# Differential attention on one core: the combination of the two exponentials of a unit made wholly by VectorE, none of it by GpSimd

## The chip, the cores and the metric

One Trainium2 chip, one of its cores. The time is that of one execution on the device, in microseconds (us); of several runs the median is given. The engines of the core are named TensorE (PE in the profile), VectorE (DVE), ScalarE (ACT), GpSimd (POOL) and SyncE (SP, which here only issues DMAs).

## The reference

Two layers; each mixes 512 latent tokens (and 256 context tokens) by three groups side by side: a recurrent one, a short convolution, and differential attention of four heads, whose part alone matters here. One input projection feeds all groups, one output projection takes their gated outputs. The attention has two score maps per head (j), of 64 channels each, and a number `lam` for each layer; behind it come a norm over the 128 channels of v and the gate:

```python
def diff_attend(q, k, v, lam, scale):
    s = jnp.einsum('bqhjd,bkhjd->bhjqk', q, k).astype(jnp.float32) * scale
    p = jax.nn.softmax(s, axis=-1)
    attn = p[:, :, 0] - lam * p[:, :, 1]
    return jnp.einsum('bhqk,bkhe->bqhe', attn.astype(v.dtype), v)
```

## The kernel before

The latent and context tokens make 6 tiles of 128 queries (layer 0), or 4 (layer 1, whose context queries are not needed). A query tile of latent tokens sees all 768 keys, one of context tokens the 256 context keys. The work of the attention is cut into units: a single unit is one latent query tile of one head, with two score rows of 768; in layer 0 the two context query tiles of a head make one more unit, with 256 keys each. The kernel has 32 single units, 16 in each layer, and 4 of two tiles. All instructions of VectorE stand at line 118, and TensorE's matmuls at line 137 and its transposes at 145, since helpers record them.

A unit passes through these stages:

- `scores`: matmuls of TensorE into PSUM (sc), each map by a high and a low part of the keys (KH, KL).
- `maxi`: VectorE takes the negative maximum of each row (mx, 128x768), one per map.
- `expo` (L1250): ScalarE writes e0 and e1, 128x768 each in SBUF, and the row sums (oden).
- `coef`: VectorE computes cf, minus `lam` times the ratio of the two row sums, in two operations of 128x1. The division by the first row sum is made later, on the output.
- `combine`: e0 + cf * e1, in place of e0. In a single unit the score columns lie so that e0 is latent keys, then context keys, and e1 is context keys, then latent keys. The 512 latent columns are one operation of VectorE (scalar_tensor_tensor). With `SP` not zero, the 256 context columns are made by GpSimd in two operations, a product (L1261) and a sum (L1262), which `coef` issues ahead of VectorE's. A unit of two tiles is combined by VectorE in either case.
- `aT_mm`, `aT_cp`: TensorE turns e0 in two halves (aTp, columns 0 to 383 and 384 to 767), ScalarE copies each out (aT, L1285). The second half needs all that was combined in the context columns.
- `av`: TensorE multiplies with the values; `drain`: ScalarE copies the output out (O, L1304) and sums its squares (osq, L1307).
- `finish`, once a head: VectorE's small operations oss, rs_i, rs_y, rs_t and ors (a reciprocal root by iteration), GpSimd's product O*ors (L1325), TensorE's transposes of O (oT), VectorE's product with the gate (zT), and the split of the result into a rounded part (ScalarE, L1338) and the rest (GpSimd, L1339; VectorE for the last head).

`attention` runs over the units as a hand-made pipeline: at step x it turns and multiplies unit x, combines unit x+1, takes the exponentials of unit x+2 and the scores and maxima of unit x+3; `finish` of a head is put at the second and the fourth unit of the next head. The operations of the pipeline are kept in the order of their own code on VectorE and on ScalarE. The operations of `finish`, the splits of weights for the output projection (wraw into wo..hi by ScalarE, L265, and wo..lo by VectorE or GpSimd, L268) and the end of the input projection (lat, qkr, qks) are put between them by a scheduler, by its own estimate of when each engine is free.

The two functions that hold the choice read:

```python
            if m == 1 and SP:
                e0, e1 = u["e", 0][:, NL:], u["e", 1][:, :NC]
                G.tensor_tensor(out=e1, in0=e1, in1=cf[:, 0:1].to_broadcast([P, NC]), op=ALU.mult)
                G.tensor_tensor(out=e0, in0=e0, in1=e1, op=ALU.add)

        def combine(u):
            cf, e0, e1 = u["cf"], u["e", 0], u["e", 1]
            if len(u["tt"]) == 1:
                pr = [(e0[:, :NL], e1[:, NC:], 0)] + ([] if SP else [(e0[:, NL:], e1[:, :NC], 0)])
```

Of the kernel before, what the change touches and what calls it, by code (L numbers as in the profile page):

```python
# [45 lines left out]
YE = 0  # L46
YS = 0
TP = 1
SP = 256
AL = 1  # L50
EB = (3,2)
ATB = 2
# [54 lines left out]
def build(tc, A):  # L107
# [1080 lines left out]
    def attention(l, lat, cx, pool, az_done, hd0):  # L1188
# [64 lines left out]
        def coef(u):  # L1253
# [4 lines left out]
                                      op0=ALU.mult, op1=ALU.mult))  # L1258
            if m == 1 and SP:
                e0, e1 = u["e", 0][:, NL:], u["e", 1][:, :NC]  # L1260
# [3 lines left out]
# [4 lines that stand above are left out]
            else:  # L1268
# [464 lines left out]
```

## Time and profile before

| | us |
|---|---|
| median of 3 runs | 1144.48 |
| the three runs | 1138.93, 1144.48, 1145.29 |
| the profiled execution, its own time | 1140.77 |
| span of the profile | 1139.0 |

The span is the time from the first to the last instruction that the profile records. The attention of layer 0 lies between some 470 and 567 us of it, that of layer 1 between some 1010 and 1085 us; before each lies the input projection, behind each the output projection. The shares of busy time over the whole span say little of these two stretches, so they are read by stretch. An instruction's duration in the trace includes what it waits for inside the engine; bracketed idle time is what the engine stood idle before it.

### The profile page before, as it was taken

What the parts mean: (1) busy time and instruction counts of PE and PEld (TensorE: products, weight loads), DVE (VectorE), ACT (ScalarE), POOL (GpSimd) and SP (SyncE); (2) the same over time, 40 slices, a digit from 0 to 9 for tenths busy, and PEclk for the clock granted to TensorE, in tenths of its full rate; (3) what the DMA queues carried; (4) which work ended last, traced back from release to release, by engine and by line L of the source; (5) the groups of instructions that cost most, each with busy time, mean ns of one, the idle gap of its engine ahead of it and who ended that gap; (6) DMA issues with size and microseconds to landing.
All of it is one profiled execution on the core that took longest, in us unless ns stands there. A gap on an engine that the chain in (4) does not pass through costs nothing.

```text
span 1139.0 us, 25449 instructions
## 1 busy us (share of the span) xinstructions
PE 1030.2 (90%) x9850; PEld 843.0 (74%) x9850; DVE 723.5 (64%) x1704; ACT 523.3 (46%) x1330; POOL 500.2 (44%) x516
## 2 busy tenths in 40 slices
PE   4899989999699999988899999998988999888897
PEld 1567968777689867877787776866767897768775
DVE  3530558688467261599747867766985815479944
ACT  3432553453362323478724664654344433248731
POOL 0311534434727522555522346254475463456522
PEclk9999999999899999999999999999999999999999
DMA  9574321112424456654052352222223345555143
GB/s 355 177 242 131 87 77 56 59 33 85 138 76 124 144 179 195 192 172 103 18 186 93 130 194 71 84 86 74 79 68 107 98 142 150 158 168 160 48 157 110
DMA packets 92088, 142.55 MB, mean 125 GB/s; under 512 B 28192, under 2 KB 36416, under 8 KB 91968
## 3 DMA queue, kind: packets, MB, share of 16 engines
q1 hardware_dynamic: 88512, 136.14, 38.1%
q10 hardware_dynamic: 3456, 4.80, 1.3%
q8 instruction: 77, 1.26, 0.5%
q14 instruction: 43, 0.35, 0.1%
HBM read 110.99 MB, written 25.71 MB: 120 GB/s over the span
## 4 chain that ended last, share of the span: by engine, by line
PE 35%; DVE 22%; ACT 6%; POOL 6%; issue 4%; DMA 4%; SPq 1%; DVEq 0%; POOLq 0%; ACTq 0%
PE pcl L137 11%; PE op L137 6%; DVE mx L118 4%; PE ptl L137 3%; PE pcc L137 3%; PE ptc L137 2%; DVE e L118 2%; DVE rs_t L118 2%; DMA mraw<-in_mod_w_dram 2%; DVE bk L118 1%; PE ch L135 1%; PE av L137 1%; POOL wlo L268 1%; DVE qkr L118 1%; PE yps L135 1%
## 5 line engine op out<-in xcount | busy, mean ns | idle before, releaser
L268 POOL TENSOR_TENSOR wlo<-wraw,whi 128x512 fp32r<-128x512 f32 x134 | 182.3, 1364 | 304.6 <-ACT whi L265 272.8
L137 PE MATMUL pcl<-lat,whi 128*128 128x512 f32 (+1 forms) x928 | 295.5, 395 | 2.6 <-issue 1.6
L137 PEld LDWEIGHTS pcl<-lat,whi 128*128 128x128 f32 x928 | 170.8, 191 | 40.5 <-issue 7.5
L137 PE MATMUL pcl<-lat,wlo 128*128 128x512 f32 (+1 forms) x464 | 185.5, 400 | 3.8 <-POOL wlo L268 3.8
L265 ACT CAST whi<-wraw 128x512 fp32r<-128x512 f32 x144 | 88.7, 619 | 151.8 <-DMA wraw<-in_w_in_dram 45.6
L137 PE MATMUL pcc<-ctx,whi 128*128 128x256 f32 x576 | 111.3, 290 | 1.8 <-DVE ctx L118 1.7
L137 PEld LDWEIGHTS pcl<-lat,wlo 128*128 128x128 f32 x464 | 88.2, 190 | 28.3 <-POOL wlo L268 5.7
L137 PEld LDWEIGHTS pcc<-ctx,whi 128*128 128x128 f32 x576 | 94.0, 195 | 8.6 <-issue 3.2
L137 PE MATMUL pcc<-ctx,wlo 128*128 128x256 f32 x288 | 83.8, 291 | 1.9 <-DVE wlo L118 1.9
L137 PE MATMUL ptl<-whi,lat 128*128 128x256 f32 x384 | 80.1, 295 | 0.0
L1250 ACT ACTIVATE e<-sc,mx 128x768 f32<-128x768 f32 (+1 forms) x80 | 66.3, 832 | 19.5 <-DVE mx L118 14.1
L137 PE MATMUL av<-vA,aT 128*128 128x128 f32 x416 | 59.7, 287 | 14.0 <-ACT aT L1285 13.9
L118 DVE TENSOR_REDUCE mx<-sc 128x1 f32<-128x768 f32 (+1 forms) x72 | 63.7, 919 | 12.4 <-PE sc L137 12.3
L137 PEld LDWEIGHTS av<-vA,aT 128*128 128x128 f32 x416 | 54.5, 196 | 20.9 <-ACT aT L1285 17.9
L137 PEld LDWEIGHTS ptl<-whi,lat 128*128 128x128 f32 x384 | 63.8, 197 | 2.0 <-issue 0.4
L118 DVE TENSOR_TENSOR R<-s,cs 128x384 f32<-128x384 f32 (+1 forms) x96 | 47.0, 529 | 20.2 <-PE s L135 19.4
L137 PEld LDWEIGHTS pcc<-ctx,wlo 128*128 128x128 f32 x288 | 56.0, 194 | 4.7 <-DVE wlo L118 2.3
L947 POOL TENSOR_TENSOR pz<-zu,pc 64x128 f32<-64x128 f32 x88 | 39.4, 448 | 42.1 <-DVE zu L118 37.4
L137 PE MATMUL ptl<-wlo,lat 128*128 128x256 f32 x192 | 56.5, 295 | 0.0
L137 PE MATMUL sc<-KH,QS 128*128 128x256 f32 (+1 forms) x144 | 50.9, 367 | 4.7 <-ACT e L1250 2.9
L1261 POOL TENSOR_TENSOR e<-e,cf 128x256 f32<-128x256 f32 x32 | 26.3, 822 | 42.0 <-DVE rs_y L118 13.3
L137 PE MATMUL sc<-KL,QS 128*128 128x256 f32 (+1 forms) x144 | 44.6, 332 | 0.0
(450 smaller groups left out, 2446.8 us busy)
## 6 DMA issues: line engine op xcount, KB each, us to landing
wraw<-in_w_in_dram SPq DMA_DIRECT2D x144, 256.0 KB, 2.7
mraw<-in_mod_w_dram SPq DMA_DIRECT2D x96, 256.0 KB, 4.5
KH<-qd SPq DMA_DIRECT2D x32, 192.0 KB, 3.6
oraw<-in_w_out_dram SPq DMA_DIRECT2D x20, 256.0 KB, 4.0
qd<-qks SPq DMA_DIRECT2D x12, 384.0 KB, 2.4
qd<-qkr SPq DMA_DIRECT2D x12, 384.0 KB, 2.7
qks<-qkr SPq DMA_DIRECT2D x64, 64.0 KB, 2.1
zu<-vd SPq DMA_DIRECT2D x96, 32.0 KB, 2.2
```

The costliest lines, as they stand in the source:

```text
L118: i = f(*a, **k)
L135: tc.keep_in_program_order(nc.tensor.matmul(*a, **k))
L137: i = nc.tensor.matmul(*a, **k)
L265: S.copy(hi, raw)
L268: eng.tensor_tensor(out=lo, in0=raw, in1=hi.bitcast(F32), op=ALU.subtract)
L947: G.tensor_tensor(out=pz[d][hr], in0=zu[d][hr, :, h, :], in1=prepd[d][1][hr, :, cc[d][1]].unsqueeze(2).to_broadcast([64, 2, HD]), op=ALU.mult)
L1250: ac(S.activation(ej[:, c], pb[:, c], AF.Exp, bias=mx[:, i:i + 1], accum_out=den[:, u["h"] * 6 + tt, j:j + 1]))
L1261: G.tensor_tensor(out=e1, in0=e1, in1=cf[:, 0:1].to_broadcast([P, NC]), op=ALU.mult)
```

## The change

The constant `SP` (line 49) is what `coef` and `combine` ask for:

```diff
-SP = 256
+SP = 0
```

With 0, `coef` issues nothing to GpSimd, so L1261 and L1262 are gone (64 instructions of 128x256). `combine` issues a second scalar_tensor_tensor of VectorE for each single unit, over the 256 context columns, right behind that over the 512 latent ones (32 instructions of 128x256). No data moves to another place, and no buffer changes.

TensorE's instructions keep their order. On VectorE, ScalarE, GpSimd and SyncE the order changes in the attention of the two layers and nowhere else, since the scheduler places what lies between the pipeline's operations anew. Three places follow; the numbers behind e and r are names of buffers.

VectorE in layer 0, where head 0 is finished while head 1's units run (ors is the root's last product, by which GpSimd scales O; r its reciprocal row sum; zT the gated output of the transposed O). Before:

```order
L118 SCALAR_TENSOR_TENSOR rs_t<-rs_t,oss 128x6
L118 SCALAR_TENSOR_TENSOR ors<-rs_t,rs_y 128x6
L118 TENSOR_REDUCE mx<-sc 128x1
L118 TENSOR_TENSOR ors<-ors,r_6196 128x6
L118 TENSOR_REDUCE mx<-sc 128x1
L118 RECIPROCAL cf<-oden 128x1
L118 RECIPROCAL r_6473<-oden 128x6
L118 SCALAR_TENSOR_TENSOR cf<-cf,lm_579,oden 128x1
L118 SCALAR_TENSOR_TENSOR e_6243<-e_6256,cf,e_6243 128x512
L118 TENSOR_REDUCE mx<-sc 128x2 x2
L118 RECIPROCAL cf<-oden 128x1
L118 SCALAR_TENSOR_TENSOR cf<-cf,lm_579,oden 128x1
```

and after:

```order
L118 SCALAR_TENSOR_TENSOR rs_t<-rs_t,oss 128x6
L118 TENSOR_TENSOR wo21lo<-wraw,wo21hi 128x512
L118 SCALAR_TENSOR_TENSOR ors<-rs_t,rs_y 128x6
L118 SCALAR_TENSOR_TENSOR e_6236<-e_6249,cf,e_6236 128x512
L118 TENSOR_TENSOR ors<-ors,r_6190 128x6
L118 SCALAR_TENSOR_TENSOR e_6236<-e_6249,cf,e_6236 128x256
L118 TENSOR_REDUCE mx<-sc 128x2 x2
L118 TENSOR_TENSOR zT<-oT,zT 128x384 x2
L118 RECIPROCAL cf<-oden 128x1
L118 SCALAR_TENSOR_TENSOR cf<-cf,lm_579,oden 128x1
L118 SCALAR_TENSOR_TENSOR e_6277<-e_6310,cf,e_6277 128x512
L118 SCALAR_TENSOR_TENSOR e_6277<-e_6310,cf,e_6277 128x256
```

Behind each combination of 128x512 stands one of 128x256; the weight split wo21lo has come ahead of the combination, the product of ors and r, which GpSimd's scaling of O waits for, has moved from before the maxima of the previous unit to behind the combination, and both zT stand ahead of the next one.

VectorE in layer 1, around the combination of the second unit of head 2, where head 1's root is computed. Before:

```order
L118 SCALAR_TENSOR_TENSOR cf<-cf,lm_588,oden 128x1
L118 TENSOR_TENSOR oss<-oss,r_12978 128x4
L118 SCALAR_TENSOR_TENSOR e_12855<-e_12868,cf,e_12855 128x512
L118 TENSOR_SCALAR oss<-oss 128x4
L118 TENSOR_SCALAR rs_i<-oss 128x4
L118 TENSOR_SCALAR rs_y<-rs_i 128x4
L118 TENSOR_TENSOR rs_t<-rs_y 128x4
L118 SCALAR_TENSOR_TENSOR rs_t<-rs_t,oss 128x4
L118 SCALAR_TENSOR_TENSOR rs_y<-rs_t,rs_y 128x4
L118 TENSOR_TENSOR rs_t<-rs_y 128x4
L118 TENSOR_REDUCE mx<-sc 128x1 x2
L118 RECIPROCAL cf<-oden 128x1
```

and after:

```order
L118 TENSOR_TENSOR wo01lo<-wraw,wo01hi 128x512
L118 SCALAR_TENSOR_TENSOR cf<-cf,lm_588,oden 128x1
L118 TENSOR_TENSOR oss<-oss,r_12951 128x4
L118 SCALAR_TENSOR_TENSOR e_12830<-e_12843,cf,e_12830 128x512
L118 SCALAR_TENSOR_TENSOR e_12830<-e_12843,cf,e_12830 128x256
L118 TENSOR_SCALAR oss<-oss 128x4
L118 TENSOR_REDUCE mx<-sc 128x1 x2
L118 RECIPROCAL cf<-oden 128x1
L118 TENSOR_SCALAR rs_i<-oss 128x4
L118 TENSOR_TENSOR wo11lo<-wraw,wo11hi 128x512
L118 SCALAR_TENSOR_TENSOR cf<-cf,lm_588,oden 128x1
L118 TENSOR_SCALAR rs_y<-rs_i 128x4
```

The root's chain (rs_i, rs_y, rs_t) stood whole between this combination and the next maxima, and now comes behind those maxima; two weight splits, wo01lo and wo11lo, stand ahead of two combinations here, where before they came later.

ScalarE at the same place, where the exponentials alternate with the copies of aT. Before:

```order
L1285 COPY aT<-aTp 128x384
L1250 ACTIVATE e_12868,oden<-sc,mx 128x768
L1304 COPY O<-av 128x128
L1307 ACTIVATE osq,oss<-av 128x128
L1338 CAST lat_112<-zT 128x512
L1285 COPY aT<-aTp 128x384
L1250 ACTIVATE e_12910,oden<-sc,mx 128x768
L1285 COPY aT<-aTp 128x384
L1250 ACTIVATE e_12923,oden<-sc,mx 128x768
L265 CAST wo01hi<-wraw 128x512
L1304 COPY O<-av 128x128
```

and after:

```order
L1285 COPY aT<-aTp 128x384
L1250 ACTIVATE e_12843,oden<-sc,mx 128x768
L1304 COPY O<-av 128x128
L1307 ACTIVATE osq,oss<-av 128x128
L265 CAST wo01hi<-wraw 128x512
L265 CAST wo10hi<-wraw 128x512
L1338 CAST lat_112<-zT 128x512
L1285 COPY aT<-aTp 128x384
L1250 ACTIVATE e_12884,oden<-sc,mx 128x768
L1285 COPY aT<-aTp 128x384
L1250 ACTIVATE e_12897,oden<-sc,mx 128x768
```

The roundings of three weight blocks (wo01hi, wo10hi, wo11hi) have come forward, the first two ahead of the rounding of lat, which waits for zT.

## Rows read from the trace of the kernel before

**Rows 1.** The head of the profile's page: the span, then busy time, its share of the span and the number of instructions of each engine.

```profile
span 1139.0 us, 25449 instructions
...
PE 1030.2 (90%) x9850; PEld 843.0 (74%) x9850; DVE 723.5 (64%) x1704; ACT 523.3 (46%) x1330; POOL 500.2 (44%) x516
```

**Rows 2.** Busy time of each engine in two stretches: the attention of layer 0 (490 to 570 us) and that of layer 1 (990 to 1085 us). Columns: length, busy us and instructions of TensorE matmul, its weight load, VectorE, ScalarE and GpSimd, granted TensorE clock, DMA share, GB/s.

```profile
490.00:570.00 80.00, 69.31 (x481) 61.07 (x481) 70.12 (x165) 62.25 (x202) 43.99 (x48) 0.98 0.33 93
...
990.00:1085.00 95.00, 80.83 (x531) 70.69 (x529) 78.72 (x154) 60.98 (x163) 54.78 (x53) 0.98 0.40 122
```

**Rows 3.** The chain that ended last, by line, in the attention of layer 0 (465 to 590 us) and then in that of layer 1 (1000 to 1090 us).

```profile
by line: DVE mx L118 18.4%; PE op L137 17.4%; DVE e L118 9.1%; PE av L137 5.6%; ACT e L1250 4.7%; issue 4.4%; PE pcl L137 4.2%; DVE qkr L118 3.8%; DVE rs_t L118 3.6%; PE sc L137 3.0%; PE aTp L145 2.9%; POOL qks L1124 2.8%; ACT aT L1285 2.3%
...
by line: DVE mx L118 21.8%; DVE qkr L118 10.3%; issue 9.6%; PE av L137 8.5%; DVE e L118 8.0%; PE op L137 4.9%; PE sc L137 3.5%; DVE lat L118 3.2%; ACT e L1250 3.2%; PE aTp L145 3.0%; PE pcl L137 2.6%; DVE cf L118 2.4%; POOL qks L1124 1.9%; 
```

**Rows 4.** Groups of instructions, shapes kept apart: first of 490 to 570 us, then of 985 to 1085 us. Columns: line, engine, operation, output and inputs, shapes, count; busy us in total and mean ns of one; idle time before them and what ended it.

```profile
L118 DVE TENSOR_REDUCE mx<-sc 128x1 f32<-128x768 f32 x28 | 25.6, 949 | 1.7 <-PE sc L137 1.5
...
L118 DVE SCALAR_TENSOR_TENSOR e<-e,cf,e 128x512 f32<-128x512 f32 x15 | 14.1, 940 | 0.4
L1262 POOL TENSOR_TENSOR e<-e,e 128x256 f32<-128x256 f32 x15 | 13.3, 884 | 0.9
...
L1261 POOL TENSOR_TENSOR e<-e,cf 128x256 f32<-128x256 f32 x15 | 12.2, 816 | 20.2 <-DVE rs_y L118 9.5 <-DVE rs_t L118 5.4 <-DVE cf L118 5.1
...
L118 DVE SCALAR_TENSOR_TENSOR e<-e,cf,e 128x256 f32<-128x256 f32 x6 | 2.6, 481 | 0.0
...
L118 DVE TENSOR_REDUCE mx<-sc 128x1 f32<-128x768 f32 x32 | 29.3, 948 | 7.2 <-PE sc L137 7.2
...
L118 DVE SCALAR_TENSOR_TENSOR e<-e,cf,e 128x512 f32<-128x512 f32 x16 | 15.1, 945 | 1.0 <-DVE rs_t L118 0.4
...
L1262 POOL TENSOR_TENSOR e<-e,e 128x256 f32<-128x256 f32 x16 | 14.7, 916 | 1.3
L1261 POOL TENSOR_TENSOR e<-e,cf 128x256 f32<-128x256 f32 x16 | 13.3, 833 | 20.8 <-DVE cf L118 7.0 <-DVE rs_t L118 4.3 <-DVE rs_y L118 3.8
```

**Rows 5.** All engines in order of time, of which one row of VectorE and one of GpSimd are kept: a unit of layer 0 whose combination is not stretched (start, us, engine, line, operation, output and inputs; in brackets the idle time of the engine before it and what ended it).

```profile
521.43 0.75 DVE L118 SCALAR_TENSOR_TENSOR e<-e,cf,e 128x512 f32<-128x512 f32 x1
...
521.54 1.11 POOL L1261 TENSOR_TENSOR e<-e,cf 128x256 f32<-128x256 f32 x1 [0.16 <-DVE cf L118]
```

**Rows 6.** The same view, and again VectorE's and GpSimd's rows alone, of a unit in the next head whose combination is stretched.

```profile
533.15 1.20 DVE L118 SCALAR_TENSOR_TENSOR e<-e,cf,e 128x512 f32<-128x512 f32 x1
...
533.19 0.61 POOL L1261 TENSOR_TENSOR e<-e,cf 128x256 f32<-128x256 f32 x1 [4.76 <-DVE rs_y L118]
...
533.88 1.06 POOL L1262 TENSOR_TENSOR e<-e,e 128x256 f32<-128x256 f32 x1
...
534.27 0.69 DVE L118 TENSOR_TENSOR rs_t<-rs_y 128x6 f32<-128x6 f32 x1
```

**Rows 7.** VectorE in order of time, a unit of two query tiles (two combinations of 128x256 in one row, from the first's start to the second's end) and what follows it.

```profile
529.21 0.88 DVE L118 SCALAR_TENSOR_TENSOR e<-e,cf,e 128x256 f32<-128x256 f32 x2
530.01 0.16 DVE L118 TENSOR_TENSOR oss<-oss,r 128x6 f32<-128x6 f32 x1
```

**Rows 8.** VectorE in order of time: the first and the last of the 17 stretched combinations of the program, the last with the instruction behind it (two answers). They are also the first and the last of 36 instructions of VectorE, from 476.48 to 1080.63 us, that were longer than the shortest of their kind while an L1261 or L1262 ran.

```profile
476.48 1.10 DVE L118 SCALAR_TENSOR_TENSOR e<-e,cf,e 128x512 f32<-128x512 f32 x1
...
1080.63 1.19 DVE L118 SCALAR_TENSOR_TENSOR e<-e,cf,e 128x512 f32<-128x512 f32 x1
1085.14 0.86 DVE L118 TENSOR_TENSOR zT<-oT,zT 128x384 f32<-128x384 f32 x2 [3.32 <-PE oT L145]
```

**Rows 9.** VectorE in order of time: two of the six instructions that come next but for small ones after a single unit's combination and that VectorE waited for (bracket: idle time before, and what ended it); two answers, both of layer 0, the last of the six being the last row of rows 8.

```profile
526.62 1.82 DVE L118 TENSOR_REDUCE mx<-sc 128x1 f32<-128x768 f32 x2 [0.46 <-PE sc L137]
...
563.74 0.56 DVE L118 TENSOR_TENSOR zT<-oT,zT 128x384 f32<-128x384 f32 x1 [1.73 <-PE oT L145]
```

**Rows 10.** GpSimd and TensorE in order of time (two answers of the view of all engines): the scaling of head 0's output in layer 0, the one row of L1325 in it, and the matmuls that turn that output (oT).

```profile
519.91 1.47 POOL L1325 TENSOR_TENSOR O<-O,ors 128x768 f32<-128x768 f32 x1 [1.24 <-DVE ors L118]
...
522.92 0.49 PE L145 MATMUL oT<-ident,O 128*128 128x128 f32 x3
523.98 0.55 PE L145 MATMUL oT<-ident,O 128*128 128x128 f32 x3 [0.57 <-ACT osq L1307]
```

**Rows 11.** VectorE in order of time in layer 1, behind the combination of the second unit of head 2: the first and the last of the six small operations of head 1's root (rs_i to rs_t), the maxima behind them, and a weight split.

```profile
1053.48 1.20 DVE L118 TENSOR_SCALAR rs_i<-oss 128x4 int32<-128x4 int32 x1
...
1055.52 0.16 DVE L118 TENSOR_TENSOR rs_t<-rs_y 128x4 f32<-128x4 f32 x1
1055.60 1.81 DVE L118 TENSOR_REDUCE mx<-sc 128x1 f32<-128x768 f32 x2
...
1057.46 0.68 DVE L118 TENSOR_TENSOR wo01lo<-wraw,wo01hi 128x512 fp32r<-128x512 f32 x1
```

**Rows 12.** ScalarE in order of time in the same stretch.

```profile
1051.23 0.62 ACT L1338 CAST lat<-zT 128x512 fp32r<-128x512 f32 x1 [2.04 <-DVE zT L118]
...
1057.44 0.90 ACT L1250 ACTIVATE e<-sc,mx 128x768 f32<-128x768 f32 x1 [1.75 <-DVE mx L118]
```

**Rows 13.** DMA issues of 1040 to 1066 us: what lands, queue, count, KB each, median us from issue to landing.

```profile
wraw<-in_w_out_dram SPq DMA_DIRECT2D x4, 256.0 KB, 4.3
```

**Rows 14.** The waits of each engine, added up by line, of 490 to 570 us and then of 990 to 1085 us: engine and what it waited for, us in total, times, the longest.

```profile
ACT e L1250 <- DVE mx L118: 4.4, 5, 1.5
...
ACT e L1250 <- DVE mx L118: 6.2, 6, 1.7
```

## The prediction

> **What bounds the kernel now.** The head of the page [rows 1] has TensorE busy for 90% of the span and VectorE for 64%, but that is a mean over stages, and the change touches the attention alone. So the second view is that of its two stretches [rows 2]: VectorE is busy for 70.12 of 80 us and 78.72 of 95, that is 88 and 83%; TensorE for 69.31 and 80.83, 87 and 85%; GpSimd only for 55 and 58%. Two engines are equally full, and the reader should see which of them is waited for. The chain that ended last [rows 3] has VectorE's maxima at its head in both layers (18.4 and 21.8%) and the combination behind (9.1 and 8.0%); no row of GpSimd's part of the combination is in it. The groups [rows 4] say the same: the maxima stood idle for TensorE for 1.7 us in layer 0 and 7.2 in layer 1, the combinations for 0.4 and 1.0. And ScalarE stood idle for the maxima in 11 places, 4.4 and 6.2 us [rows 14]. VectorE sets the pace, with little room before TensorE does. A microsecond of VectorE's queue here is nearly a microsecond of the span, whichever way it goes.
>
> **The change, part by part.** *What it adds.* 32 operations of 128x256 on VectorE, each right behind one of 128x512. The trace has the same form in the units of two tiles: two in a row begin at 529.21, and the next instruction at 530.01 [rows 7], so 0.40 us each, and 32 x 0.40 = 12.8 us. From above it is bounded by the mean of that group, 0.48 [rows 4], 15.4 us in all; from below by the slope between 128x256 and an undisturbed 128x512, which took 0.75 [rows 5]: 0.75 - 0.48 = 0.27, 8.7 in all. I take 0.40, since in a row is how the change issues them.
>
> [...]
>
> Behind six combinations VectorE waits anyway: the first of them for the maxima's scores, 0.46 us, another for oT, 1.73 [rows 9], the last for oT, 3.32 [rows 8]. The additions there are hidden, 6 x 0.40 = 2.4, and 10.4 us are exposed. If the moves below close those gaps, they cost 2.4 again. Queued behind each addition are the next maxima, for which ScalarE's exponentials wait.
>
> *What it removes.* GpSimd loses 12.2 + 13.3 + 13.3 + 14.7 us in 62 of its 64 instructions [rows 4], which were not on the chain. What counts is what they do to VectorE. In one unit the combination starts 0.11 us ahead of L1261, takes 0.75, and L1261 takes 1.11 [rows 5]. In another both are released by cf, L1261 is in first and takes 0.61, and the combination takes 1.20, 0.45 more; then L1262 takes 1.06, and rs_t behind the combination takes 0.69 [rows 6], where another rs_t takes 0.16 [rows 11]. So the two engines work on these tiles one at a time, and whoever comes second stands. That unit loses 0.45 + 0.53 = 0.98 us to GpSimd, more than the 0.40 that the addition costs.
>
> How often? The 15 and 16 combinations of the two groups took 14.1 + 15.1 us [rows 4], the one before them 1.10 [rows 8]: 30.3 against 32 x 0.75 = 24.0, so 6.3 us of stretch, in 17 of them. With the small operations that follow, 36 instructions of VectorE were longer than the shortest of their kind while L1261 or L1262 ran, the first at 476.48, the last at 1080.63 [rows 8], by 15.5 us together: as much as 16 units like that of rows 6. At the six places with a wait behind them 0.9 of it (the last alone has 1.19 - 0.75 = 0.44 [rows 8]) is worth nothing, which leaves 14.6.
>
> The sum of these two: 10.4 - 14.6 = **-4.2 us**.
>
> *What it moves.* Three places, by the order.
> (1) Layer 0, end of head 0: the product of ors moves behind the next combination, and wo21lo ahead of it. GpSimd's scaling of O, at 519.91 now, and the turning of O, at 522.92 and 523.98 [rows 10], come later, by at most 1.2 us (a split like wo01lo's, 0.68 [rows 11], and the 0.75 of a combination, less the small operations between), and both zT now stand ahead of the next combination. The gap before the maxima there [rows 9] takes some of it: 0 to +1.2.
> (2) Layer 1, head 1's root: from the start of rs_i at 1053.48 to the start of the maxima at 1055.60 [rows 11] VectorE did small operations while ScalarE waited 1.75 us for those maxima [rows 12]. With the chain behind the maxima, 0 to -1.75.
> (3) The same place, weight splits: wo01hi and wo10hi fall into ScalarE's idle 2.04 us ahead of the rounding of lat [rows 12], which costs nothing. But wo11lo stands ahead of a cf now, soon after wo01lo, and the blocks of wraw take turns in their buffers: if its block (256 KB, 4.3 us from issue to landing [rows 13]) is asked for when wo01lo is done at about 1052, it lands at about 1056.5, wo11hi and wo11lo follow, and that cf comes up to 1.6 us late: 0 to +1.6.
> Together -1.75 to +2.8; (2) and (3) lie in the same two units and oppose each other. I take 0.
>
> The moves left aside, the profiled execution (1140.77 us, 1.8 over its span) would come to 1136.6. The median of the three runs is 3.7 higher, so the forecast goes by it: 1144.48 - 4.2 = 1140.3, rounded to **1140**.
>
> **The rivals.**
> *VectorE pays, and the stretch of the small operations was free.* Only the combinations' own stretch, 6.3, comes back, and the small operations' (15.5 - 6.3 = 9.2) does not, because ScalarE and TensorE were no further on when they ended. For it: ScalarE waited for maxima in 11 places only [rows 14], in 32 single units. Against: the small operations stand in one queue with the maxima. It gives 10.4 - 6.3 = +4.1, with covers gone and move (1) at its worst 12.8 - 6.3 + 1.2 = +7.7: 1148.6 to 1152.2. It decides as soon as less than 10.4 us come back, 0.33 for each single unit. This is the slower side.
> [...]
> *TensorE is next.* What VectorE gains is lost again as waiting for scores and oT, since TensorE is as full as VectorE [rows 2], and the maxima waited 7.2 us for it in layer 1 already [rows 4]. Then nothing changes: about 1144.5.
> *More comes back.* The second operation costs only the slope, 8.7 us, of which a quarter-microsecond at six places, 1.6, is hidden: 7.1 - 14.6 = -7.5; with the root chain's -1.75 it is -9.2, 1135.3. For it: a following operation may overlap the end of the one before; against it, rows 7.
> That the change doesn't do what it says is excluded by the order: each single unit has the second operation, and GpSimd's two are gone.
>
> **How the numbers follow.** 0.5% is about what a measurement of this kernel can tell from no change: 5.7 us. The forecast's case spans -2 to -6.5 (the price from 0.27 to 0.48 is partly in the rival above, the moves are +-1.5) and has 0.48: 0.08 beyond 0.5%, 0.40 within. TensorE next: 0.14, within. More comes back: 0.15, faster. VectorE pays: 0.23, of which 0.15 beyond and 0.08 within. Faster 0.23, same 0.62, slower 0.15. The range goes down to the third rival with two more microseconds for the median's own spread (1138.93 to 1145.29), 1133, and up into the slower rival, 1151, which leaves out about 0.1 above and less below.
>
> **What would show it.** In the two stretches VectorE's group of 128x256 has 6 + 31 instructions instead of 6, at 0.40 to 0.48; the mean of the 128x512 falls from 0.94 to about 0.75; no rs_t of 0.69 stands behind a combination. The last zT of layer 0 (563.74 now) and of layer 1 (1085.14) come about 2 us earlier each, counted from the stage's start. The prediction is wrong if the 128x512 fall to 0.75 and yet these ends don't come earlier (TensorE next, then the idle time before the maxima grows beyond 1.7 and 7.2 us), if the small operations stay long behind other work of GpSimd, or if wo11lo or the late O opens a gap of over 1.5 us ahead of a cf or zT.

## The result and the profile after

Ratio of the changed kernel to the kernel before 0.9949, 95% interval 0.9928 to 0.9971, from 22 runs of each (medians 1137.46 and 1143.81 us), of which one of the kernel before, at 4715.63 us, is left out of the ratio: -5.8 us, between -8.2 and -3.3. Here and below a difference in us is the ratio less one, times the median of the kernel before, run beside it. The profiled execution took 1136.55 us.

The head of the page of the changed kernel, then its two stretches (length, busy us and instructions of TensorE, its weight load, VectorE, ScalarE and GpSimd, granted clock, DMA share, GB/s):

```profile
span 1134.8 us, 25347 instructions
...
PE 1029.8 (91%) x9850; PEld 844.0 (74%) x9850; DVE 714.8 (63%) x1736; ACT 523.7 (46%) x1330; POOL 446.5 (39%) x452
```

```profile
490.00:570.00 80.00, 70.63 (x480) 62.67 (x479) 69.02 (x186) 61.45 (x200) 18.91 (x17) 0.96 0.36 100
990.00:1085.00 95.00, 82.14 (x538) 72.24 (x537) 81.39 (x183) 61.98 (x165) 28.12 (x22) 0.98 0.40 119
```

Against [rows 1] GpSimd lost 64 instructions and 53.7 us, and VectorE, which got 32 more, is busy for 8.7 us *less*. Only about half of that lies in the two attention stages. Before and after, from the first combination to the zT at the end of each stage (columns as above):

```profile
476.48:563.74 87.26, 75.42 (x521) 66.90 (x519) 80.74 (x173) 66.75 (x212) 50.55 (x52) 0.98 0.37 107
1012.44:1085.14 72.70, 59.65 (x411) 52.28 (x411) 64.23 (x137) 54.30 (x152) 42.99 (x45) 0.98 0.36 108
```

```profile
475.72:562.21 86.49, 76.17 (x521) 68.19 (x519) 76.69 (x189) 66.53 (x212) 25.10 (x20) 0.96 0.38 108
1010.58:1081.21 70.63, 59.19 (x411) 52.46 (x411) 64.12 (x152) 54.45 (x152) 15.64 (x13) 0.98 0.38 111
```

VectorE fell there from 144.97 to 140.82 us, by 4.2, although it got 31 instructions more: they cost less than the standing still that it lost. The rest of the 8.7 lies where the program did not change. In [rows 2]'s stretches GpSimd fell from 55 and 58% to 24 and 30%. TensorE shows 1.3 us more in each of them: in layer 1 the stretch holds 7 more of its instructions; in layer 0 it holds one less, at a mean granted clock of 0.96 instead of 0.98. For 6.8 us of it the clock was 0.50, in the first answer here, and 1.00 ahead of that (490.00 to 501.00) and behind (507.80 to 570.00); the second answer is the wait of TensorE as it fell (both of the changed kernel):

```profile
501.00:507.80 6.80, 6.24 (x24) 5.58 (x25) 5.58 (x14) 4.74 (x18) 0.00 (x0) 0.50 0.89 246
```

```profile
501.52 0.79 PE L137 MATMUL av<-vA,aT 128*128 128x128 f32 x2 [2.61 <-ACT aT L1285]
```

The groups of VectorE, first of 490 to 570 us, then of 985 to 1085 us (count; busy us, mean ns of one; idle time before them):

```profile
L118 DVE TENSOR_REDUCE mx<-sc 128x1 f32<-128x768 f32 x27 | 24.7, 951 | 2.2 <-PE sc L137 2.2
...
L118 DVE SCALAR_TENSOR_TENSOR e<-e,cf,e 128x512 f32<-128x512 f32 x15 | 11.3, 750 | 0.2
...
L118 DVE SCALAR_TENSOR_TENSOR e<-e,cf,e 128x256 f32<-128x256 f32 x21 | 10.3, 502 | 0.0
...
L118 DVE TENSOR_REDUCE mx<-sc 128x1 f32<-128x768 f32 x32 | 29.4, 950 | 6.9 <-PE sc L137 6.9
...
L118 DVE SCALAR_TENSOR_TENSOR e<-e,cf,e 128x512 f32<-128x512 f32 x16 | 12.0, 752 | 0.2
...
L118 DVE SCALAR_TENSOR_TENSOR e<-e,cf,e 128x256 f32<-128x256 f32 x16 | 9.5, 592 | 0.0
```

The combination of 128x512 fell from 940 and 945 ns [rows 4] to 750 and 752: none of the 32 is stretched any more. The 128x256, of which the two-tile units have 6 in the first stretch, cost 502 and 592 ns; what exceeds 480 ns is three of them, which stand beside L353, L1339 and L1325 of GpSimd for 0.48, 1.04 and 0.78 us. A unit in order of time, VectorE:

```profile
1060.40 0.75 DVE L118 SCALAR_TENSOR_TENSOR e<-e,cf,e 128x512 f32<-128x512 f32 x1
1061.07 0.16 DVE L118 TENSOR_TENSOR rs_t<-rs_y 128x4 f32<-128x4 f32 x1
1061.14 0.48 DVE L118 SCALAR_TENSOR_TENSOR e<-e,cf,e 128x256 f32<-128x256 f32 x1
1061.54 0.16 DVE L118 SCALAR_TENSOR_TENSOR rs_t<-rs_t,oss 128x4 f32<-128x4 f32 x1
```

From the start of the 128x256 (1061.14) to the next instruction (1061.54) are 0.40 us, and rs_t behind the combination takes 0.16, where it took 0.69 in [rows 6]. The other GpSimd work is still in the way, here L268 and L1339, at the place of [rows 11] and [rows 12]; VectorE and GpSimd (two answers), then ScalarE:

```profile
1049.94 1.17 DVE L118 TENSOR_TENSOR oss<-oss,r 128x4 f32<-128x4 f32 x1
...
1051.64 1.23 DVE L118 SCALAR_TENSOR_TENSOR cf<-cf,lm,oden 128x1 f32<-128x1 f32 x1
...
1055.90 0.68 DVE L118 TENSOR_TENSOR wo11lo<-wraw,wo11hi 128x512 fp32r<-128x512 f32 x1
...
1049.80 1.28 POOL L268 TENSOR_TENSOR wo10lo<-wraw,wo10hi 128x512 fp32r<-128x512 f32 x1 [1.24 <-ACT wo10hi L265]
1051.05 1.80 POOL L1339 TENSOR_TENSOR lat<-zT,lat 128x512 fp32r<-128x512 f32 x1
```

```profile
1049.99 0.62 ACT L1338 CAST lat<-zT 128x512 fp32r<-128x512 f32 x1 [0.26 <-DVE zT L118]
...
1053.76 0.62 ACT L265 CAST wo11hi<-wraw 128x512 fp32r<-128x512 f32 x1 [0.61 <-DMA wraw<-in_w_out_dram]
...
1055.89 0.90 ACT L1250 ACTIVATE e<-sc,mx 128x768 f32<-128x768 f32 x1 [0.70 <-DVE mx L118]
```

ScalarE's wait for zT fell from 2.04 to 0.26 us, since two roundings now fill it, and that for the maxima from 1.75 to 0.70; the block of weights came 0.61 us late for wo11hi, and wo11lo on VectorE did not wait. At the end of head 0 in layer 0 (VectorE, GpSimd and TensorE, three answers), to be read against [rows 10]:

```profile
520.75 0.69 DVE L118 TENSOR_TENSOR wo21lo<-wraw,wo21hi 128x512 fp32r<-128x512 f32 x1 [0.52 <-ACT wo21hi L265]
...
522.09 0.16 DVE L118 TENSOR_TENSOR ors<-ors,r 128x6 f32<-128x6 f32 x1
...
524.61 1.02 DVE L118 TENSOR_TENSOR zT<-oT,zT 128x384 f32<-128x384 f32 x2 [0.77 <-PE oT L145]
...
522.33 1.64 POOL L1325 TENSOR_TENSOR O<-O,ors 128x768 f32<-128x768 f32 x1 [6.15 <-DVE ors L118]
...
524.03 0.87 PE L145 MATMUL oT<-ident,O 128*128 128x128 f32 x6 [1.06 <-POOL O L1325]
```

The weight split waits 0.52 us for its rounding with the combination behind it, O is scaled at 522.33 instead of 519.91, and oT is 1.1 us later; counted from the first combination of the stage, which comes 0.76 us earlier here, these are 3.2 and 1.9 us. Last, the zT near the ends of the two stages, with their first combinations: the changed kernel's, and the one row of before that is not shown yet:

```profile
475.72 1.14 DVE L118 SCALAR_TENSOR_TENSOR e<-e,cf,e 128x512 f32<-128x512 f32 x2
...
562.21 0.56 DVE L118 TENSOR_TENSOR zT<-oT,zT 128x384 f32<-128x384 f32 x1 [0.56 <-issue]
...
1010.58 1.15 DVE L118 SCALAR_TENSOR_TENSOR e<-e,cf,e 128x512 f32<-128x512 f32 x2
...
1081.21 0.86 DVE L118 TENSOR_TENSOR zT<-oT,zT 128x384 f32<-128x384 f32 x2 [3.10 <-issue]
```

```profile
1012.44 0.75 DVE L118 SCALAR_TENSOR_TENSOR e<-e,cf,e 128x512 f32<-128x512 f32 x1
```

From the first combination to zT, layer 0 took 563.74 - 476.48 = 87.3 us [rows 8, 9] and takes 86.5; layer 1 took 1085.14 - 1012.44 = 72.7 [rows 8] and takes 70.6. So 2.9 us of the 4.2 by which the spans differ lie in the attention, three quarters of them in layer 1. The other 1.3 lie where the program did not change. (These zT are not the last of their layers, as the prediction has it: those of the last head begin at 576.48 and 1094.48 before, at 574.94 and 1090.56 after, and give the same 0.8 and 2.1 us.)

### The profile page after: what moved, and what is told of

It is laid out like the page before. It is cut to its first block, busy times and chain, and to the rows that moved or that the text cites. A ratio compares the mean times of both kernels' runs of the same rounds, so it can differ in the third digit from the quotient of the medians.

```text
span 1134.8 us, 25347 instructions
## 1 busy us (share of the span) xinstructions
PE 1029.8 (91%) x9850; PEld 844.0 (74%) x9850; DVE 714.8 (63%) x1736; ACT 523.7 (46%) x1330; POOL 446.5 (39%) x452
## 4 chain that ended last, share of the span: by engine, by line
PE 41%; DVE 15%; ACT 7%; issue 6%; POOL 6%; DMA 3%; SPq 1%; ACTq 0%; DVEq 0%; POOLq 0%
PE pcl L137 14%; PE op L137 6%; PE ptl L137 3%; PE pcc L137 3%; PE av L137 2%; PE ptc L137 2%; PE sc L137 2%; DVE mx L118 2%; PE ch L135 1%; DMA mraw<-in_mod_w_dram 1%; ACT e L1250 1%; DVE bk L118 1%; DVE rs_t L118 1%; PE yps L135 1%; POOL wlo L268 1%
## 5 line engine op out<-in xcount | busy, mean ns | idle before, releaser
L268 POOL TENSOR_TENSOR wlo<-wraw,whi 128x512 fp32r<-128x512 f32 x134 | 181.6, 1358 | 303.1 <-ACT whi L265 261.6
L1250 ACT ACTIVATE e<-sc,mx 128x768 f32<-128x768 f32 (+1 forms) x80 | 66.3, 831 | 15.9 <-DVE mx L118 10.4
L118 DVE COPY zu<-ch 64x128 f32<-64x128 f32 x48 | 14.1, 294 | 47.8 <-ACT zu L968 41.8
```

Of the source, the lines that this page charges most:

```text
L118: i = f(*a, **k)
L268: eng.tensor_tensor(out=lo, in0=raw, in1=hi.bitcast(F32), op=ALU.subtract)
L1250: ac(S.activation(ej[:, c], pb[:, c], AF.Exp, bias=mx[:, i:i + 1], accum_out=den[:, u["h"] * 6 + tt, j:j + 1]))
```

## The experiments

Each is an edit of the changed kernel unless its expectation says otherwise. The ratio is to the kernel before, run beside it.

| run | ratio (95% interval) | us against before |
|---|---|---|
| the change | 0.9949 (0.9928 to 0.9971) | -5.8 |
| neither | 0.9864 (0.9833 to 0.9895) | -15.6 |
| both | 1.0102 (1.0068 to 1.0137) | +11.7 |
| twice | 1.0060 (1.0031 to 1.0089) | +6.9 |
| product | 1.0029 (0.9999 to 1.0059) | +3.3 |
| first | 0.9992 (0.9962 to 1.0021) | -0.9 |
| second | 0.9969 (0.9942 to 0.9997) | -3.6 |
| late | 0.9936 (0.9906 to 0.9967) | -7.3 |
| wide | 0.9950 (0.9929 to 0.9972) | -5.7 |
| split | 1.0000 (0.9976 to 1.0024) | 0.0 |
| turned | 0.9954 (0.9920 to 0.9987) | -5.3 |
| scaled | 1.0009 (0.9977 to 1.0041) | +1.0 |
| turned_scaled | 0.9964 (0.9933 to 0.9994) | -4.1 |

### The theory's two terms: neither, both, twice, product

The theory is the forecast's: additions of 10.4 us against 14.6 of standing still, both on the path. The rival: only the combinations' own stretch counts. The second rival: TensorE is the bound.

**neither**

```diff
-                pr = [(e0[:, :NL], e1[:, NC:], 0)] + ([] if SP else [(e0[:, NL:], e1[:, :NC], 0)])
+                pr = [(e0[:, :NL], e1[:, NC:], 0)]
```

> Neither engine combines the 256 context columns of the single units: GpSimd's two operations are gone, as in the change, and VectorE's second operation is left out too (so the context keys of the single units count by the first softmax alone). VectorE, ScalarE, TensorE and SyncE keep their order of before word for word, so this is GpSimd's work taken away and nothing else. By the forecast's theory (GpSimd holds VectorE up for 15.5 us, and nearly all of it is on the path) -14.6 us against before, ratio 0.987. If only the combinations' own stretch counts and that of the small operations was free: -6.3, 0.9945. If TensorE is the next bound and cuts the gain off: about the changed kernel's time, -5.8, 0.995, with long idle times of VectorE before the maxima.

**both** (for product, the last line is left out)

```diff
+        g0 = pool.tile([P, NC], F32, name="g0")
+        g1 = pool.tile([P, NC], F32, name="g1")
+        G.memset(g0, 1.0)
+        G.memset(g1, 1.0)
...
+            if m == 1:
+                G.tensor_tensor(out=g1, in0=g1, in1=cf[:, 0:1].to_broadcast([P, NC]), op=ALU.mult)
+                G.tensor_tensor(out=g0, in0=g0, in1=g1, op=ALU.add)
```

> The changed kernel, and GpSimd still runs one product and one sum of 128x256 for each single unit, on two tiles of its own that nobody reads, released by cf as before. VectorE's order is that of the changed kernel word for word. By the forecast's theory the stretch comes back in full on top of the additions: +14.6 against the changed kernel, +10.4 against before less the moves' gain (-1.6 as the measured -5.8 has it): +8.8, ratio 1.008. If only the combinations' stretch counts: +6.3 against the changed kernel, about +0.5 against before, 1.000. If the stretch counts for nothing and the moved order made the gain: as the changed kernel, 0.995.

**twice** (the same two tiles, filled by VectorE; with the added operations the order on VectorE and ScalarE moves too)

```diff
+            if len(u["tt"]) == 1:
+                dv(V.scalar_tensor_tensor(out=g0, in0=g1, scalar=cf[:, 0:1], in1=g0, op0=ALU.mult, op1=ALU.add))
```

> The changed kernel with one more VectorE operation of 128x256 behind each single unit's combination, on two tiles of its own that nobody reads. By the forecast's theory VectorE is the bound and each costs 0.40 us but where it waits anyway: +10.4 to +12.8 against the changed kernel, +4.6 to +7 against before, ratio 1.004 to 1.006. If TensorE is the bound now, most of it is hidden: +0 to +4 against the changed kernel, 0.995 to 0.9985.

**product**

> The changed kernel, and GpSimd still runs the product alone, on a tile of its own that nobody reads; the sum is gone. VectorE's order is that of the changed kernel. By the forecast's theory the product, released by cf at the same moment as the combination, holds the combination up by 0.45 us in 17 to 32 units: +7.7 to +14 against the changed kernel, 1.002 to 1.007 against before; about half of what both operations cost (+17.6 by the run with both). If only the sum, which falls among the small operations, costs time: as the changed kernel, 0.995.

Four corners come of this, with and without GpSimd's work, with and without VectorE's additions. GpSimd's work costs 15.6 us without the additions (before against neither, where no engine but GpSimd has another order) and 11.7 + 5.8 = 17.5 with them (both against the change). The additions cost 15.6 - 5.8 = 9.8 without GpSimd's work and 11.7 with it, in both cases with the moved order, and a second set of them, in an order of its own, costs 6.9 + 5.8 = 12.7. The product alone costs 3.3 + 5.8 = 9.1, about half of the pair. Against forecast terms of 14.6 and 10.4 each is within some 3 us, and both rivals are off by more than the intervals: with the first, neither is -6.3 and the interval ends at -12.0; with the second, twice hardly costs anything.

In neither GpSimd's own queue is free of the two operations as well. That this is the main gain is unlikely: in the trace of before GpSimd stood idle ahead of all its six products of O and ors in the attention (0.1 to 1.5 us), and late, below, gains 7.3 us with the work still on GpSimd.

One thing that the forecast has no term for went along with these runs, TensorE's granted clock. Its mean over the runs was 0.974 to 0.975 in the four series of the kernel before that have it, 0.976 in the change and in late, 0.979 in neither, 0.971 in twice and 0.967 in both; in the trace of both it is 0.94 and 0.96 between the times of [rows 2], where before has 0.98 and 0.98. Among the runs of one kernel a clock lower by 0.001 goes with a time longer by about 0.9 us (one slope for all kernels). By that, as an estimate, some 4 of neither's 15.6 us, 7 of both's 11.7, 3 of twice's 6.9 and 2 of the change's 5.8 go with the clock; what is left is 9 to 11 us for GpSimd's work, 5 to 8 for the additions and about -4 for the change. Whether the clock falls because TensorE waits for a slower VectorE, or apart from it, no run here tells. The signs stand either way; the sizes of the single terms are less sure than the four corners make them look.

The run both shows what the standing still looks like when it is not the combination that stands. All engines in order of time, VectorE's and GpSimd's rows (GpSimd's two are L1264 and L1265 here):

```profile
1052.65 0.75 DVE L118 SCALAR_TENSOR_TENSOR e<-e,cf,e 128x512 f32<-128x512 f32 x1
...
1052.76 1.11 POOL L1264 TENSOR_TENSOR g<-g,cf 128x256 f32<-128x256 f32 x1 [1.69 <-DVE rs_t L118]
...
1053.32 0.57 DVE L118 SCALAR_TENSOR_TENSOR rs_y<-rs_t,rs_y 128x4 f32<-128x4 f32 x1
...
1053.81 0.47 DVE L118 SCALAR_TENSOR_TENSOR e<-e,cf,e 128x256 f32<-128x256 f32 x1
1053.95 0.92 POOL L1265 TENSOR_TENSOR g<-g,g 128x256 f32<-128x256 f32 x1
1054.21 0.68 DVE L118 TENSOR_TENSOR rs_t<-rs_y 128x4 f32<-128x4 f32 x1
```

```profile
L1264 POOL TENSOR_TENSOR g<-g,cf 128x256 f32<-128x256 f32 x16 | 17.3, 1083 | 25.3 <-DVE cf L118 8.9 <-DVE rs_y L118 6.2 <-DVE rs_t L118 4.1
...
L118 DVE SCALAR_TENSOR_TENSOR e<-e,cf,e 128x512 f32<-128x512 f32 x16 | 12.4, 778 | 0.2
L118 DVE SCALAR_TENSOR_TENSOR e<-e,cf,e 128x256 f32<-128x256 f32 x16 | 12.1, 759 | 0.0
```

Here the combination is first by 0.11 us and keeps its 0.75 (mean 778 ns in the layer); the product stands for it, to 1.11; then rs_y takes 0.57 instead of 0.16, and beside the sum rs_t takes 0.68. Counted as for the forecast, 45 instructions lose 19.4 us to L1264 and L1265 in both, and 30 lose 11.5 in product, and the time rose by 17.5 and 9.1. In both about 10 us of it stand in the small operations that the first rival called free and 8.5 in the 128x256; in product it is mostly the 128x256 (6.9), so that run says little of the small ones. That their standing still counts rests on neither and both; how nearly in full, the clock leaves open.

In these rows, of two that read SBUF, the one that was first ran on and the other stood: the product ended at 1053.87, and rs_y, begun at 1053.32, at 1053.89. The maxima, which read PSUM here, show no such stretch: 949 ns in [rows 4] with GpSimd busy and 951 without its two operations. An instruction with one input stood as well: rs_i took 1.20 us in [rows 11] while L1339 ran (1.27 us from 1053.39), and 0.15 at 1055.84 in the changed kernel, with GpSimd idle.

### Where it falls: first, second

```diff
-            if m == 1 and SP:
+            if m == 1 and last:
...
-                pr = [(e0[:, :NL], e1[:, NC:], 0)] + ([] if SP else [(e0[:, NL:], e1[:, :NC], 0)])
+                pr = [(e0[:, :NL], e1[:, NC:], 0)] + ([] if last else [(e0[:, NL:], e1[:, :NC], 0)])
```

(an edit of the kernel before, that of first; second has `not last`)

> The change in layer 0 alone; layer 1 keeps GpSimd's two operations. By the forecast's theory, by the rows of before: 16 additions of 0.40, three hidden, are +5.2; 18 stretches of 7.4 us in layer 0 go: -2.2 against before, ratio 0.998. If the gain of the change came from the moved order in layer 1 alone, 1.000 or slower.

> The change in layer 1 alone; layer 0 keeps GpSimd's two operations. By the forecast's theory +5.2 for the additions and -8.0 for 18 stretches: -2.8 against before, 0.9975; with the root's chain behind the maxima up to -4.5, 0.996. If the gain came from layer 0 alone, 1.000.

-0.9 and -3.6, together -4.5, as far as intervals of 3 us tell like the whole change's -5.8; layer 1 has the larger part, as in the profile (2.1 of 2.9). Layer 0's own gain is not told from zero.

### The standing still removed without the additions: late

```diff
+            if len(u["tt"]) == 1:
+                W = NC + 1
+                G.tensor_tensor(out=e1[:, :W], in0=e1[:, :W], in1=cf[:, 0:1].to_broadcast([P, W]), op=ALU.mult)
+                G.tensor_tensor(out=e0[:, NL:], in0=e0[:, NL:], in1=e1[:, :NC], op=ALU.add)
```

(an edit of the kernel before: these lines stand behind the loop of `combine`, and those of `coef` are gone)

> The kernel before, its context columns still combined by GpSimd, but issued after VectorE's combination, and the product takes one column more (257), the first of the latent columns of e1, which the combination reads and nobody needs afterwards: so GpSimd starts when the combination ends, and where maxima come next (they read PSUM) it runs beside them. VectorE, ScalarE, TensorE and SyncE keep the order of before. By the forecast's theory the combinations' 6.3 us come back and VectorE has no additions; of the other 9 us a part stays where small operations follow instead of maxima: -6 to -13 against before, 0.989 to 0.995, at best better than the changed kernel. If the later end of the sum (about 0.4 us, or 1.3 where nothing was stretched) holds up the second half of the transposes, that is taken off again: 0.995 to 1.003.

-7.3, in the range. Three groups of late's layer 1 (1000 to 1085 us), and what TensorE's transposes waited for in 990 to 1085 us:

```profile
L118 DVE SCALAR_TENSOR_TENSOR e<-e,cf,e 128x512 f32<-128x512 f32 x16 | 12.0, 751 | 0.7
...
L1271 POOL TENSOR_TENSOR e<-e,e 128x256 f32<-128x256 f32 x16 | 11.7, 730 | 1.1
...
L1270 POOL TENSOR_TENSOR e<-e,cf 128x257 f32<-128x257 f32 x16 | 10.4, 651 | 25.2 <-DVE e L118 14.5 <-DVE rs_y L118 3.6 <-ACT aT L1285 2.3
```

```profile
PE aTp L145 <- POOL e L1271: 1.7, 3, 0.8
```

The combinations are back at 751 ns, and GpSimd's two operations, in part beside the maxima now, take 651 and 730 instead of 833 and 916 [rows 4]: a product begun at 1043.03 took 0.61 us beside two maxima of 1.81 together, as long as in [rows 11]; the maxima of this layer took 949 ns. Counted as for the forecast, 18 instructions of VectorE still lose 6.1 us to L1270 and L1271, instead of 15.5 in 36; and TensorE waits 1.7 us for the later sum here and 1.6 in layer 0 (before it waited 0.6 for it in layer 0 and not at all here). 15.5 - 6.1 - 3.3 = 6.1, or 6.7 with that 0.6, beside 7.3 measured. It is no faster than the change as far as the intervals tell (0.9906 to 0.9967 and 0.9928 to 0.9971).

### Attempts at a faster version: wide, split, turned, scaled, turned_scaled

**wide** (the second map's score columns laid as the first's, its 512 latent columns as two matmuls of 256 for the high part of the keys and two for the low, and the whole combination as one operation of 128x768)

```diff
-                segs = ([(0, tt, 0, 0), (0, tt, NL, 512), (1, tt, NL, 768)], [(1, tt, 0, 1024)])[j]
+                segs = ([(0, tt, 0, NL, 0), (0, tt, NL, NT, 512), (1, tt, 0, 256, 768)],
+                        [(1, tt, 256, NL, 1024), (1, tt, NL, NT, 1280)])[j]
...
+                pr = [(e0, e1, 0)]
```

> [...] By the slope of the rows of before an operation of 768 takes 0.75 + 0.27 = 1.02 us (start to start about 0.94) where the two take 0.67 + 0.40 = 1.07: -0.13 a unit, -4 us against the changed kernel if VectorE is the bound and the two more matmuls and weight loads per unit of TensorE are hidden. [...]

```profile
1049.00 1.02 DVE L118 SCALAR_TENSOR_TENSOR e<-e,cf,e 128x768 f32<-128x768 f32 x1
1049.93 0.16 DVE L118 SCALAR_TENSOR_TENSOR rs_y<-rs_t,rs_y 128x4 f32<-128x4 f32 x1
```

The row of wide (VectorE in order of time) has the 1.02 us expected, 0.93 to the next start, yet the time is that of the change.

**split** (as wide, but `pr = [(e0[:, :NL], e1[:, :NL], 0), (e0[:, NL:], e1[:, NL:], 0)]`)

> As the run with one operation of 128x768 (wide), the score columns of the second map laid as the first's and four matmuls of 256 in place of two of 512, but the combination again as two operations, of 128x512 and 128x256. It tells why wide was not faster than the change: if TensorE's extra instructions eat VectorE's gain of 0.13 us a unit, this is slower than wide by about 4 us, 0.9985 against before; if VectorE's gain is worth nothing, the same as wide, 0.995.

Slower than wide by 5.7 us, which pointed to the extra matmuls, though the order on VectorE and ScalarE differs between the two as well. **turned** does without them:

```diff
+                if o0 == 1024 and len(u["tt"]) == 1:
+                    kh, kl, o = (z.rearrange("p (c k) -> p c k", c=2) for z in (kh, kl, o))
+                    kh, kl = kh[:, ::-1], kl[:, ::-1]
...
+                if j == 1 and len(u["tt"]) == 1:
+                    oe, ie = (z.rearrange("p (c k) -> p c k", c=3) for z in (oe, ie))
+                    ie = ie[:, ::-1]
...
+                pr = [(e0, e1, 0)]
```

> The changed kernel with the combination as one operation of 128x768, without the extra matmuls of the run wide: the second map's latent key halves are taken by the matmul in turned order (second half first), and ScalarE reads that map's three blocks of 256 score columns backwards, so that its exponentials lie as the first map's. TensorE, ScalarE have as many instructions and columns as in the changed kernel. By the theory that VectorE is the bound, and that TensorE's extra instructions took back in wide what one operation gains (split against wide, 5 to 6 us): -4 to -6 against the changed kernel, 0.990 to 0.9915 against before. If the extra matmuls were not what wide lost, 0.995.

A miss: -5.3, where -10 to -11.5 was expected. So the extra matmuls are not shown to be what wide lost: without them the time is the same, and in turned's layer 1 the exponentials (918 ns; 910 in the change) and the matmuls of 512 columns (492; 491) take no longer for being turned. Why split is slower than the change stays open with it. One thing speaks in the trace of turned: VectorE's instructions that are longer than their shortest kind beside other GpSimd work (the products of O, the splits) lose 14.8 us in turned's attention, 11.8 in the change's, so 3.0 of the 4 gained went there. In wide they lose 11.3, so that is no general answer. Both make the first half of the transposes wait for 768 columns instead of 512, and both have another order on VectorE; what ate the gain stays open.

**scaled** and **turned_scaled**

```diff
-            E1.tensor_tensor(out=O[:, :ntt], in0=O[:, :ntt],
-                             in1=rs[:, :ntt].unsqueeze(2).to_broadcast([P, ntt, P]), op=ALU.mult)
+            if h < 3:
+                for t in range(ntt):
+                    S.activation(O[:, t], O[:, t], AF.Identity, scale=rs[:, t:t + 1])
+            else:
+                E1.tensor_tensor(out=O[:, :ntt], in0=O[:, :ntt],
+                                 in1=rs[:, :ntt].unsqueeze(2).to_broadcast([P, ntt, P]), op=ALU.mult)
```

> The changed kernel with the product of O and ors of the first three heads made by ScalarE (one operation for each query tile) in place of GpSimd. In the changed kernel VectorE still loses 3.1 us in 3 instructions to that product (L1325). If GpSimd's work on SBUF costs VectorE time whatever it is: -3 against the changed kernel, 0.992 against before; if ScalarE's 6 operations a head stand in the way of its copies and exponentials: up to +3, 0.9975.

> Both edits of the runs turned and scaled: if each works as the theory has it, they add up to -7 to -9 against the changed kernel, 0.987 to 0.989 against before; if TensorE is the bound by then, no faster than turned alone.

Misses too: scaled is 6.8 us slower than the change although 3.1 us of standing still behind L1325 are gone, and turned_scaled is no faster than turned. ScalarE's operations in its one queue, and the order, which moved on VectorE and ScalarE, are both candidates; no run tells them apart.

## Why the prediction was right

- *VectorE sets the pace*: shown in sign. Work put on it costs time (twice, 12.7 for 32 operations of 0.40), and time taken from it comes back (neither, -15.6, with its order unchanged). That the cost is the length of the operations and no more is not shown, since the granted clock moved too.
- *The additions, 10.4*: 9.8, 11.7 and 12.7 in three comparisons, each of them with another order as well. 0.40 us each, from the row of the two-tile units, was right; 0.27, the slope, holds inside one instruction (1.02 for 768), not for a second one behind it. That 2.4 of the 12.8 would be hidden is not told apart by these runs. For the -6.5 at the far end of the forecast's case no run shows a term; the row has 0.40 an addition and the runs 9.8 to 12.7 us for 32.
- *The standing still, 14.6*: 15.6 and 17.5, with intervals that hold 14.6, and of these some 4 and 7 us go with the clock. It was read from durations of the trace alone, 36 instructions longer than the shortest of their kind, and neither confirms that it is on the path, with the other engines' order unchanged. In the traces, one each, the two stages to the last zT are 11.5 us shorter in neither than before, and 15.4 longer in both than in the change.
- *The moves, 0*: not separated. One cost more than its bound of 1.2: in layer 0 O is scaled 2.4 us later and oT 1.1 (3.2 and 1.9 from the stage's start), since the product of ors also moved behind a maximum and a cf, which the bound left out. In layer 1 ScalarE's idle time ahead of the maxima fell by 1.05 us and that for zT by 1.78, filled by the two roundings, and the late block cost 0.61 instead of 1.6. A version with the changed kernel's order and without its additions was not tried.
- *The sum, -4.2*: -5.8 (-8.2 to -3.3), of which about 2 go with a clock that the forecast did not reckon with. The two terms are of 10 and 15 us and each is good to some 3 at best, so the closeness of their difference is in part luck.
- *The signs*: the 128x512 fell to 750 and 752 ns. The idle time before the maxima went from 1.7 to 2.2 and from 7.2 to 6.9, and VectorE waited 0.77 for oT behind the late O, so two of the signs of being wrong stayed away. The third came in part: behind other work of GpSimd VectorE's instructions still lose 11.8 us.
- *The ends 2 us earlier each*: layer 1 yes (2.1), layer 0 not (0.8). There the late O and TensorE's clock (0.96 instead of 0.98) are both candidates for the rest; no run tells them apart.
- *VectorE pays*, the slower rival: fell with neither and both. *TensorE is next*: fell with neither, which goes 10 us further. *More comes back*: its price of 0.27 is against the row of the changed kernel (0.40 from start to start) and against twice.

## What to carry to other kernels

Before moving work from a full VectorE to GpSimd, look whether both read SBUF at that moment, as they did here: 0.40 us of VectorE work a unit was saved for about 0.5 us of standing still, much of it in small operations of 0.16 us that took 0.6 to 0.7 and in no row of the moved work. Compare each instruction's duration with the shortest of its kind and sum the excess by what GpSimd did meanwhile; that sum was the larger of the two terms here, though by how much it counts was read only to a few us. If GpSimd is to keep the work, release it when VectorE turns to operations on PSUM, as late does in part (its maxima stayed at 949 ns, GpSimd's two operations fell to 651 and 730): it gained as much as the change with VectorE's order untouched.

## What the runs showed that was not expected

An instruction that is first by 0.11 us keeps its own time and the loss moves to the next one: in both the combinations of 128x512 in layer 1 took 0.78 us in the mean, and the run was the slowest of all. So the stretch of the combinations, by itself, says little of what GpSimd costs. And edits that took work from VectorE or GpSimd in equal measure (turned, scaled) differed by 6 us, as much as the change itself is worth. The order by the scheduler, ScalarE's added operations in scaled and the granted clock are candidates for that; no run tells them apart.
